# A fused decoder layer on one core: attention probabilities turned by VectorE and DMAs, an earlier last gate, smaller recurrence tiles, and side work that may lag further

## The chip, the cores and the metric

The kernel runs on one core of one Trainium2 chip. The metric is device time in microseconds (us) of one execution. The names of the engines are those of the profile: PE is TensorE (matmul; PEld its weight load), DVE is VectorE, ACT is ScalarE, POOL is GpSimd, SP is SyncE, whose queue here only issues DMAs.

## The reference

One layer of a decoder over 256 positions and 2048 channels, in float32. One wide product of the normalised input gives everything that three branches and the gates need. Cut to its core:

```python
hn = rms_norm(h, ln_gain[l])
z = split_columns(hn @ w_in[l] + b_in[l])
y_a = rglru_branch(z['lru_x'], ...) * silu(z['lru_gate'])          # linear recurrence
y_b = nsa_branch(q_b, k_c, v_c, k_s, v_s, k_w, v_w, g_b) * silu(z['nsa_gate'])   # sparse attention, 8 heads
y_c = fox_branch(q, k, v, log_f) * silu(z['fox_gate'])             # attention with forget bias, 8 heads
mg = sigmoid(z['merge']).reshape(b, s, 3, D_MODEL)
merged = (mg[:, :, 0] * (y_a @ w_branch[l, 0])
          + mg[:, :, 1] * (y_b @ w_branch[l, 1])
          + mg[:, :, 2] * (y_c @ w_branch[l, 2]))
h = h + merged @ w_out[l]
e = rms_norm(p[l] @ w_ple[l], ple_gain[l])
h = h + sigmoid(h @ w_ple_gate[l]) * e
```

In the two attention branches softmax probabilities of a block of 128 queries are multiplied with the values. For the sparse branch there are a window part and a selected part (each 128 or 256 keys wide, for the first and the second block of queries) and a small compressed part.

## The kernel before, in words

**Products.** Every float32 operand is held as two parts, a high part (names ending in h: `wh`, `k_yh`, `k_hnh`) and a low part (`wl`, `k_yl`, `k_hnl`), and a product is three matmuls: high by high, high-of-weight by low, low by high. The weights are read once as a stream of some 390 "halves" of at most 128 x 1024 numbers. SP loads a half into `raw` (5 buffers); ACT copies it into `wh`, DVE subtracts to get `wl` (4 buffers of each, three halves ahead of use, in `cut`); PE then does 12 matmuls of 128x512 on it (`by_rows`), into one of two pairs of PSUM banks (`main`). This stream is PE's main work, and `plan()` (lines 88 to 150) writes its order out: the recurrence's inputs and gate, the sparse attention's inputs with its gate, then 12 merge chunks `c`, each with its gate product (`merge`) and its branch product (`proj`), four chunks per branch, then the output product and the last gate. The forgetting attention's inputs come before the merge chunk 4. Each `proj` half names which quarter of the split branch output `ysplit0` to `ysplit2` it needs.

**Side work.** Everything else is written as Python generators that are woven into that stream (`Side`): `lru_task` (4 of them, the recurrence), `nsa_task` (8, sparse attention, two heads and one block of 128 queries each), `fox_task` (8, one head each), `turn_chunk` (a gate or the recurrence input turned to channels on partitions), `y_split` (a branch output times its gate, split into `k_yh` and `k_yl` in four pieces). At each half and in the middle of it, `tick` lets tasks emit their next instructions, first the urgent ones and then the others, as long as a planner's estimate says that DVE and ACT lag behind PE by no more than `LIMITS`, 3.0 us for urgent tasks and 2.0 for the others. When a half needs something that isn't emitted yet (`need`), tasks are run regardless. `room` and `give` count tiles of three pools (`k4`: 4 KB per partition, 5 tiles; `k2`: 11 tiles; `k1`: 8 tiles), `settle` lets PE go on until other engines should be done, `landed` waits 7 us of planned time for a DMA. All of this is decided when the program is built; on the chip each engine runs its own list in order. All instructions are recorded by one helper and so bear line 206 in the profile; the tiles tell them apart.

**Turning.** There are two ways to transpose. On PE, a 128x128 block is multiplied with the identity into a PSUM bank (`bank<-cst,...` in the profile). Or `cross`: DVE turns all 32x32 blocks of a tile in one instruction into `zt`, and four DMAs on SP's queue move the blocks in runs of 128 bytes to where they belong. In `before`, `cross` serves the gates, the recurrence input, the keys, the queries and the merged sum; the probabilities are turned on PE. `cells` and `celled` are views of a tile in the order in which `cross` needs it.

**The start.** `row_scales` sums the squares of the input over the partitions with small matmuls on a tile of ones, and raises the result to the power of minus a half on POOL; the first chunks wait for the outcome, `rsr`.

Of the kernel before, what the change touches and what calls it, by code (L numbers as in the profile page):

```python
# [76 lines left out]
def plan():  # L77
# [50 lines left out]
    for c in range(12):  # L128
        b, j = divmod(c, 4)
        if c == 4:  # L130
            for i, r in enumerate(rows(5, N_SIDE)):
                if i == 0:
                    r[0]["starts"] = ("ysplit1",)
                out += r
        for i, q in enumerate(rows(N_SIDE + c, N_SIDE + c + 1)):
            if j == 0 and b != 1:
                q[0]["starts"] = (f"ysplit{b}",)
            out += q
        out += item("proj", c, 8, 512, ("w_branch", b, [(512 * j, 512)]),
                    needs=lambda k, b=b: (f"ysplit{b}{k // 2}",))  # L140
# [183 lines left out]
def block_kernel(ctx: ExitStack, tc: tile.TileContext, io):  # L324
# [54 lines left out]
    def split(hi, lo, src, scale=None):  # L379
        splits((hi, lo, src, scale))  # L380
# [102 lines left out]


    A.activation(sml([P, 8], name="tbl"), half_n, AF.Copy)
    def issue_x(h, k=0, n=2):

        if "pair" in h:
            i = h["pair"]
            if i + k == 0:  # L490
                Q.dma_start(x0, io["x0"])
            else:
                Q.dma_start(x_pair(i)[:, k:k + n, :], io["xT"][:, 2 * i + k:2 * i + k + n])
# [62 lines left out]
    def row_scales(acc):  # L556

        yield from side.settle()
        b, = yield from side.take()
        for t in range(NT):  # L560
            for i in range(2):
                T.matmul(banks[b][:, 2 * t:2 * t + 2], acc[:, i, t * P:(t + 1) * P], ones[:, :2],
                         start=i == 0, stop=i == 1)
        yield True
        r = sml([P, 4], name="rsc")
        rsqrt(r, banks[b][:, :4], D)
        side.back(b)
        yield from side.powers()
        V.tensor_copy(rsr, r.rearrange("p (t i) -> p t i", i=2)[:, :, 0])

# [85 lines left out]

    def cross(dst, src):


        zt = mid([P, 4, 8, 32], name="zt")  # L660
        if type(src) is list:
# [13 lines left out]
    def turn_chunk(read, out, into, dst, k0, name):  # L675
# [37 lines left out]
    def lru_task(i):  # L713
        yield from side.wait("vec", f"lru_x{i // 2}")
        yield from side.room(k2=4, k4=2)
        u = st["u"]
# [26 lines left out]
        for c in range(2):  # L743
            for s in range(2):
# [3 lines left out]
                T.matmul(g, wdl[:, c, s, :], ucs[c][:, s, :], start=False, stop=True)  # L748
        side.give(k4=2)
        yield True  # L750
# [131 lines left out]
    def nsa_task(g, pr, t):  # L882
# [10 lines left out]
        G.memset(pc3, 0.0)  # L893
        p = mid([P, 2, 2, n * P], name="prob")

        def soft(a, sc):

            for i, (o, x, msk) in enumerate(zip((pc[:, a, :], p[:, a, 0, :], p[:, a, 1, :]), sc,
                                                (cmask[:, t, :], mask[:, P * (2 - n):2 * P], mask[:, P:P + n * P]))):
# [36 lines left out]
        at = [banks[bs[0]][:, :256], banks[bs[0]][:, 256:]] if t == 0 else [banks[x] for x in bs]  # L936
# [58 lines left out]
    def fox_task(h):  # L995
        c = h // 4
        yield from side.wait(f"fq{c}", f"fk{c}", f"fv{c}", "forget", "vec")
        fq, fk, fv = st["fq"], st["fk"], st["fv"]
        yield from side.room(k1=5, k2=2)
        nck = one([P, S], name="nck")  # L1000
# [12 lines left out]
        side.give(k1=5)  # L1013
        p = two([P, 3 * P], name="fprob")
        m, s = sml([P, 2], name="fm"), sml([P, 2], name="fs")
        cols = (slice(0, P), slice(P, 3 * P))
        for t in range(NT):
            V.tensor_tensor_reduce(p[:, cols[t]], banks[b][:, cols[t]], bias[:, cols[t]], -1.0, FLOOR,
                                   OP.add, OP.min, m[:, t:t + 1])
            A.activation(p[:, cols[t]], p[:, cols[t]], AF.Exp, bias=m[:, t:t + 1], scale=-1.0, accum_out=s[:, t:t + 1])  # L1020
        side.back(b)
        side.give(k2=1)
        yield True
        yield from side.room(k1=2, k2=2)
        V.tensor_scalar(s, s, 1e-30, None, op0=OP.max)
        V.reciprocal(s, s)
        for t in range(NT):
            V.tensor_scalar(p[:, cols[t]], p[:, cols[t]], s[:, t:t + 1], None, op0=OP.mult)
        vh, vl = (one([P, S], R32, name="fx") for _ in range(2))
        split(vh, vl, fv[:, h].rearrange("p t d -> p (t d)"))  # L1030
        yield from side.settle()
        b, = yield from side.take()

        for i in range(3):
            T.transpose(banks[b][:, i * P:(i + 1) * P], p[:, i * P:(i + 1) * P], ident)
        yield True
        pth, ptl = two([P, 3 * P], R32, name="fpth"), two([P, 3 * P], R32, name="fptl")
        split(pth, ptl, banks[b][:, :3 * P])
        side.back(b)
        side.give(k2=1)  # L1040
# [214 lines left out]
    for i, h in enumerate(halves):  # L1255
# [11 lines left out]
        if "pair" in h:  # L1267
            squares(h["pair"], xacc)
            if h["pair"] == 7:
                side.urge("rs", row_scales(xacc))  # L1270
        if i == 5:
# [70 lines left out]
LAND = 7000.0  # L1342
LIMITS = 3000.0, 2000.0

# [76 lines left out]
```

## Time and profile before

| what | value |
|---|---|
| median of 3 runs | 1092.37 us (1091.62 to 1093.23) |
| profiled execution, its own time | 1091.14 us |
| its span | 1089.4 us |
| mean granted clock | 0.993 |
| DVE busy | 762.3 us (70%) |
| ACT busy | 612.3 us (56%) |
| DMA packets, of these under 512 B | 159368, 103097 |

A row of a group has the operation, out<-in and how often it occurs, then its busy time, the mean of one in ns, and the idle time before it with what ended that. A timeline row has start, duration, what, and in brackets the idle time before it with what ended it. A row of the table by stretches has, after the stretch, its length, then the busy time of PE, PEld, DVE, ACT and POOL with the number of instructions, then the granted clock, the DMA share and GB/s. Matmuls overlap, so the cost of one is the distance from its start to the next start, not its duration.

### The profile page before, as it was taken

To read this page: it belongs to the slowest core of one execution; us is meant where nothing else is said; L and a number is where in the kernel's file an instruction comes from. 1 tells how busy PE (TensorE), PEld (TensorE's weight loads), DVE (VectorE), ACT (ScalarE), POOL (GpSimd) and SP (SyncE) were. 2 spreads that over 40 slices of the span, in tenths; PEclk is the share of its full clock that TensorE was granted. 3 is DMA by queue.
4 is the path that set the end of the run, shared out by engine and by line. 5 is a ranking of instruction groups with operands and counts; after the bars stand their busy time and mean duration, and the time that the engine had idled before them with its cause. 6 is when DMAs were issued, how large, how long until landed. Compare 5 with 4: busy or idle time off the path is not lost.

```text
span 1089.4 us, 14109 instructions
## 1 busy us (share of the span) xinstructions
PE 1069.4 (98%) x5019; PEld 892.5 (82%) x5019; DVE 762.3 (70%) x1119; ACT 612.3 (56%) x912; POOL 52.1 (5%) x77
## 2 busy tenths in 40 slices
PE   9999999999979999999999999999989999999998
PEld 8788898878768888888888888888868888888886
DVE  7787788977676678677787855565665666676654
ACT  7569975587855556554555544455554544444442
POOL 0000001100000000011110000000000100000000
PEclk9999999999989999999999999999989999999999
DMA  9767868878746556459667566777747887888772
GB/s 338 227 212 242 252 201 267 268 225 230 209 128 188 168 165 175 145 158 274 201 205 224 188 193 185 231 222 213 211 136 246 248 257 210 238 239 253 270 230 78
DMA packets 159368, 232.82 MB, mean 214 GB/s; under 512 B 103097, under 2 KB 104257, under 8 KB 159297
## 3 DMA queue, kind: packets, MB, share of 16 engines
q1 hardware_dynamic: 154576, 216.16, 64.6%
q0 software_dynamic: 4720, 15.76, 5.1%
q8 instruction: 39, 0.64, 0.3%
q14 instruction: 33, 0.26, 0.1%
HBM read 215.62 MB, written 4.20 MB: 202 GB/s over the span
## 4 chain that ended last, share of the span: by engine, by line
PE 90%; ACT 2%; DVE 1%; issue 1%; DMA 0%; SPq 0%; ACTq 0%; DVEq 0%
PE main L206 84%; PE bank L206 5%; ACT wh L206 1%; DVE wl L206 0%; DMA raw<-in_w 0%; SPq L206 0%; ACT k_th L206 0%; ACT k_lru L206 0%; ACT L206 0%; DVE k_mg L206 0%; ACT k_gn L206 0%; DVE k_fin L206 0%; ACT k_yh L206 0%; DVE k_fq L206 0%; ACT k_gf L206 0%
## 5 line engine op out<-in xcount | busy, mean ns | idle before, releaser
L206 DVE TENSOR_TENSOR wl<-raw,wh 128x1024 fp32r<-128x1024 f32 (+2 forms) x388 | 462.3, 1201 | 273.7 <-ACT wh L206 272.2
L206 ACT ACTIVATE wh<-raw 128x1024 fp32r<-128x1024 f32 (+2 forms) x388 | 400.8, 1040 | 343.7 <-PE main L206 282.9
L206 PE MATMUL main<-wh,k_hnh 128*128 128x512 f32 (+2 forms) x1026 | 396.4, 387 | 0.9 <-ACT k_z L206 0.9
L206 PE MATMUL main<-wl,k_hnh 128*128 128x512 f32 (+2 forms) x1026 | 393.1, 384 | 0.5 <-DVE wl L206 0.4
L206 PE MATMUL main<-wh,k_hnl 128*128 128x512 f32 (+1 forms) x1024 | 392.5, 383 | 0.0
L206 PEld LDWEIGHTS main<-wh,k_hnh 128*128 128x128 f32 x1026 | 193.0, 188 | 37.5 <-ACT k_z L206 1.8
L206 PEld LDWEIGHTS main<-wh,k_hnl 128*128 128x128 f32 x1024 | 192.3, 188 | 38.0
L206 PEld LDWEIGHTS main<-wl,k_hnh 128*128 128x128 f32 x1026 | 193.1, 189 | 36.7 <-DVE wl L206 1.5
L206 PE MATMUL main<-wh,k_yh 128*128 128x512 f32 x192 | 77.0, 401 | 12.9 <-ACT k_yh L206 12.9
L206 PE MATMUL main<-wl,k_yh 128*128 128x512 f32 x192 | 76.3, 398 | 0.0
L206 PE MATMUL main<-wh,k_yl 128*128 128x512 f32 x192 | 76.2, 397 | 0.0
L206 PEld LDWEIGHTS main<-wh,k_yh 128*128 128x128 f32 x192 | 37.1, 193 | 21.1 <-ACT k_yh L206 13.7
L206 PE MATMUL main<-wh,k_mth 128*128 128x512 f32 x128 | 49.8, 389 | 0.0
L206 PE MATMUL main<-wl,k_mth 128*128 128x512 f32 x128 | 49.8, 389 | 0.0
L206 PE MATMUL main<-wh,k_mtl 128*128 128x512 f32 x128 | 49.8, 389 | 0.0
L206 PE MATMUL main<-wh,k_hth 128*128 128x512 f32 x128 | 49.8, 389 | 0.0
L206 PE MATMUL main<-wl,k_hth 128*128 128x512 f32 x128 | 49.8, 389 | 0.0
L206 PE MATMUL main<-wh,k_htl 128*128 128x512 f32 x128 | 49.8, 389 | 0.0
L206 PEld LDWEIGHTS main<-wh,k_yl 128*128 128x128 f32 x192 | 37.0, 192 | 8.3 <-DVE k_yl L206 0.4
L206 PEld LDWEIGHTS main<-wl,k_yh 128*128 128x128 f32 x192 | 37.1, 193 | 7.7
L206 ACT ACTIVATE k_mg<-k_mg 128x512 f32<-128x512 f32 x24 | 15.1, 632 | 25.3 <-DVE k_mg L206 25.1
L206 PEld LDWEIGHTS main<-wl,k_mth 128*128 128x128 f32 x128 | 24.0, 188 | 5.0
(249 smaller groups left out, 964.2 us busy)
## 6 DMA issues: line engine op xcount, KB each, us to landing
raw<-in_w SPq DMA_DIRECT2D x369, 512.0 KB, 4.4
bias<-in_b_in POOLq DMA_DIRECT2D x21, 256.0 KB, 4.1
raw<-in_w SPq DMA_DIRECT2D x8, 408.0 KB, 4.0
e_dram<-k_e POOLq DMA_DIRECT2D x4, 512.0 KB, 3.6
k_merged<-k_zt SPq DMA_DIRECT2D x16, 128.0 KB, 3.4
k_xc<-in_x POOLq DMA_DIRECT2D x4, 512.0 KB, 5.3
k_hx<-k_zt SPq DMA_DIRECT2D x16, 128.0 KB, 3.6
k_ec<-e_dram POOLq DMA_DIRECT2D x4, 512.0 KB, 7.6
```

Source lines behind the costliest of these rows:

```text
L206: r = call(out, *args, **kw)
```

## The change

1. **Probabilities by `cross`.** In `nsa_task` and `fox_task` the exponentials are written in cell order (`k_pz`, `k_fpz`), scaled there, and turned by `cross`, with the old probability tile as the blocks' buffer; the 72 transposes on PE go (4 tasks x 4, 4 x 8, and 8 x 3), and 16 DVE turns and 64 DMAs on SP's queue come. The high and low parts of the probabilities are then made from SBUF instead of PSUM, in one instruction where there were two. A sparse task takes two `k4` tiles at its start instead of one, a forgetting one three `k2` tiles instead of two.
2. **The last gate sooner.** `fox_gate`'s two chunks come behind merge chunk 6 instead of 7.
3. **Recurrence tiles.** The gate weights `wd` of a `lru_task` move from the `k4` pool to `k2`; the task waits for one `k4` tile instead of two.
4. **Limits.** 4.5 us for urgent tasks and 4.0 for the others.
5. **The start.** The first input `x0` is requested on ACT's queue instead of SP's. `squares` runs one half sooner. `row_scales` adds the two halves of the squares on DVE first and does two ones-matmuls instead of four (each float32 one is two PE instructions), and POOL writes `rsr` directly. `turn_chunk` emits its two copies without a break between.

```diff
-        if c == 7:
+        if c == 6:
             out += turned("fox_gate", needs=[f"fox{i}" for i in range(8)])
...
+    A.dma_start(x0, io["x0"])
+
...
     def row_scales(acc):
+        V.tensor_tensor(acc[:, 0, :], acc[:, 0, :], acc[:, 1, :], op=OP.add)
         yield from side.settle()
         b, = yield from side.take()
         for t in range(NT):
-            for i in range(2):
-                T.matmul(banks[b][:, 2 * t:2 * t + 2], acc[:, i, t * P:(t + 1) * P], ones[:, :2],
-                         start=i == 0, stop=i == 1)
-        yield True
-        r = sml([P, 4], name="rsc")
-        rsqrt(r, banks[b][:, :4], D)
+            T.matmul(banks[b][:, 2 * t:2 * t + 2], acc[:, 0, t * P:(t + 1) * P], ones[:, :2], start=True, stop=True)
+        yield True
+        rsqrt(rsr, banks[b][:, :4].rearrange("p (t i) -> p t i", i=2)[:, :, 0], D)
...
-        yield from side.room(k2=4, k4=2)
+        yield from side.room(k2=4, k4=1)
...
-        wd = mid([P, 2, 2, P], name="wd")
+        wd = two([P, 2, 2, P], name="wd")
...
-        yield from side.room(k1=3, k4=1)
+        yield from side.room(k1=3, k4=2)
...
-        p = mid([P, 2, 2, n * P], name="prob")
+
+        p, pz = mid([P, 4, 4 * n, 32], name="prob"), mid([P, 4, 4 * n, 32], name="pz")
...
-            for i, o in enumerate((pc[:, a, :], p[:, a, 0, :], p[:, a, 1, :])):
-                A.activation(o, o, AF.Exp, bias=m[:, a, i:i + 1], scale=-1.0, accum_out=s[:, a, i:i + 1])
+            for i, (o, x) in enumerate(((pc[:, a, :], pc[:, a, :]), (cell[:, a, 0], cells(ps[:, a, 0, :])),
+                                        (cell[:, a, 1], cells(ps[:, a, 1, :])))):
+                A.activation(o, x, AF.Exp, bias=m[:, a, i:i + 1], scale=-1.0, accum_out=s[:, a, i:i + 1])
...
-                V.tensor_scalar(p[:, a, w, :], p[:, a, w, :], s[:, a, 1 + w:2 + w], None, op0=OP.mult)
+                V.tensor_scalar(cell[:, a, w], cell[:, a, w], s[:, a, 1 + w:2 + w], None, op0=OP.mult)
+        pt = pz.rearrange("p b n j -> p (b n j)")
+        yield from cross(pt, pt, p)
+        side.give(k4=1)
         yield from side.room(k4=2)
-        yield from side.settle()
-        bs = yield from side.take(n)
...
-        for a in range(2):
-            for i in range(2 * n):
-                c = i % n * P
-                T.transpose(at[a][:, i * P:(i + 1) * P], p[:, a, i // n, c:c + P], ident)
-        yield True
...
-        splits(*((pth[:, :, a, :], ptl[:, :, a, :], at[a].rearrange("p (i q) -> p i q", q=P), None) for a in range(2)))
-        side.back(*bs)
+        split(*(x.rearrange("p i a q -> p (i a q)") for x in (pth, ptl)), pt)
...
-LIMITS = 3000.0, 2000.0
+LIMITS = 4500.0, 4000.0
```

`fox_task` changes in the same way as `nsa_task`.

How the order of instructions moves, at three places. First ACT before the first branch's product, in `before`; `k_mg` is the tanh of merge chunk 0, `k_th` and `k_gn` the sparse branch's gate, `k_yh` the pieces of the first branch:

```order
L206 ACTIVATE k_mg_2904<-k_mg_2904 128x512
L206 ACTIVATE k_mg_2905<-k_mg_2905 128x512
L206 ACTIVATE wh_2912<-raw_2819 128x1024
L206 ACTIVATE k_th_2916<-k_gn_2499,vec 128x256
L206 ACTIVATE k_gn_2499<-k_gn_2499,vec 128x256
L206 ACTIVATE k_th_2920<-k_gn_2499,vec 128x256
L206 ACTIVATE k_gn_2499<-k_gn_2499,vec 128x256
L206 ACTIVATE k_yh_2924<-k_yl_558 128x512
```

The first piece stands behind the tanh pair, a weight copy and four gate instructions. The same stretch of ACT in the changed kernel, from the third piece on:

```order
L206 ACTIVATE k_yh_2791<-k_yl_559 128x512
L206 ACTIVATE wh_2870<-raw_2802 128x1024
L206 ACTIVATE k_th_2886<-k_gn_2542,vec 128x256
L206 ACTIVATE k_gn_2542<-k_gn_2542,vec 128x256
L206 ACTIVATE k_th_2890<-k_gn_2542,vec 128x256
L206 ACTIVATE k_gn_2542<-k_gn_2542,vec 128x256
L206 ACTIVATE wh_2896<-raw_2829 128x1024
L206 ACTIVATE wh_2914<-raw_2847 128x1024
```

Three pieces now stand ahead of the gate and of the tanh pair (which follows, after four more gate instructions); the fourth comes two weight copies behind that pair. Second, ACT before the third branch's product in `before`, where `k_mg` is the tanh of merge chunk 8:

```order
L206 ACTIVATE k_yh_2924<-k_fq_4375 128x512
L206 ACTIVATE wh_7012<-raw_6937 128x1024
L206 ACTIVATE k_mg_7028<-k_mg_7028 128x512
L206 ACTIVATE k_mg_7029<-k_mg_7029 128x512
L206 ACTIVATE wh_7036<-raw_6963 128x1024
L206 ACTIVATE wh_7054<-raw_6989 128x1024
L206 ACTIVATE k_yh_2924<-k_fq_4375 128x512 x3
```

One piece comes ahead of the tanh pair and three behind it. In the changed kernel:

```order
L206 ACTIVATE k_yh_2791<-k_fq_4333 128x512 x2
L206 ACTIVATE wh_6928<-raw_6858 128x1024
L206 ACTIVATE k_yh_2791<-k_fq_4333 128x512
L206 ACTIVATE wh_6951<-raw_6884 128x1024
L206 ACTIVATE k_yh_2791<-k_fq_4333 128x512
L206 ACTIVATE wh_6972<-raw_6902 128x1024
L206 ACTIVATE wh_6990<-raw_6926 128x1024
L206 ACTIVATE wh_7008<-raw_6949 128x1024
L206 ACTIVATE wh_7026<-raw_6970 128x1024
L206 ACTIVATE k_mg_7042<-k_mg_7042 128x512
```

All four pieces stand ahead of the tanh pair, with four weight copies between. Third, SP's queue early in the sparse attention of the changed kernel, where `before` has weight loads alone:

```order
L206 DMA raw_3087<-in_w 128x1024
L206 DMA k_pz_2643<-k_prob_2642 128x4x32 x4
L206 DMA raw_3127<-in_w 128x1024
L206 DMA raw_3145<-in_w 128x1024
L206 DMA raw_3163<-in_w 128x1024
L206 DMA k_pz_2656<-k_prob_2655 128x8x32 x4
L206 DMA raw_3189<-in_w 128x1024
```

The four DMAs of a cross stand between weight loads, three loads apart here.

More of the change, by code (lines that the diff above doesn't have):

```diff
@@ L489, in issue_x @@
             i = h["pair"]
-            if i + k == 0:
-                Q.dma_start(x0, io["x0"])
-            else:
+            if i + k:
                 Q.dma_start(x_pair(i)[:, k:k + n, :], io["xT"][:, 2 * i + k:2 * i + k + n])
@@ L560, in row_scales @@
         for t in range(NT):
-            for i in range(2):
-                T.matmul(banks[b][:, 2 * t:2 * t + 2], acc[:, i, t * P:(t + 1) * P], ones[:, :2],
-                         start=i == 0, stop=i == 1)
+            T.matmul(banks[b][:, 2 * t:2 * t + 2], acc[:, 0, t * P:(t + 1) * P], ones[:, :2], start=True, stop=True)
         yield True
-        r = sml([P, 4], name="rsc")
-        rsqrt(r, banks[b][:, :4], D)
+        rsqrt(rsr, banks[b][:, :4].rearrange("p (t i) -> p t i", i=2)[:, :, 0], D)
         side.back(b)
         yield from side.powers()
-        V.tensor_copy(rsr, r.rearrange("p (t i) -> p t i", i=2)[:, :, 0])
     hn = [(big([P, 8, S], R32, name="hnh"), big([P, 8, S], R32, name="hnl")) for _ in range(2)]
@@ L655, in celled, with cross @@
         return [z[:, :, :, t, :] for t in range(NT)]
-    def cross(dst, src):
-        zt = mid([P, 4, 8, 32], name="zt")
+    def cross(dst, src, zt=None):
+        if zt is None:
+            zt = mid([P, 4, 8, 32], name="zt")
         if type(src) is list:
@@ L748, in lru_task @@
                 T.matmul(g, wdl[:, c, s, :], ucs[c][:, s, :], start=False, stop=True)
-        side.give(k4=2)
+        side.give(k4=1)
         yield True
@@ L893, in nsa_task @@
         G.memset(pc3, 0.0)
-        p = mid([P, 2, 2, n * P], name="prob")
+        p, pz = mid([P, 4, 4 * n, 32], name="prob"), mid([P, 4, 4 * n, 32], name="pz")
+        ps = p.rearrange("p b n j -> p (b n j)").rearrange("p (a w k) -> p a w k", a=2, w=2)
+        cell = pz.rearrange("p b (w k a) j -> p a w b k j", w=2, a=2)
         def soft(a, sc):
-            for i, (o, x, msk) in enumerate(zip((pc[:, a, :], p[:, a, 0, :], p[:, a, 1, :]), sc,
+            for i, (o, x, msk) in enumerate(zip((pc[:, a, :], ps[:, a, 0, :], ps[:, a, 1, :]), sc,
                                                 (cmask[:, t, :], mask[:, P * (2 - n):2 * P], mask[:, P:P + n * P]))):
                 V.tensor_tensor_reduce(o, x, msk, -1.0, FLOOR, OP.add, OP.min, m[:, a, i:i + 1])
-            for i, o in enumerate((pc[:, a, :], p[:, a, 0, :], p[:, a, 1, :])):
-                A.activation(o, o, AF.Exp, bias=m[:, a, i:i + 1], scale=-1.0, accum_out=s[:, a, i:i + 1])
+            for i, (o, x) in enumerate(((pc[:, a, :], pc[:, a, :]), (cell[:, a, 0], cells(ps[:, a, 0, :])),
+                                        (cell[:, a, 1], cells(ps[:, a, 1, :])))):
+                A.activation(o, x, AF.Exp, bias=m[:, a, i:i + 1], scale=-1.0, accum_out=s[:, a, i:i + 1])
         if t == 0:
@@ L931, in nsa_task @@
             for w in range(2):
-                V.tensor_scalar(p[:, a, w, :], p[:, a, w, :], s[:, a, 1 + w:2 + w], None, op0=OP.mult)
+                V.tensor_scalar(cell[:, a, w], cell[:, a, w], s[:, a, 1 + w:2 + w], None, op0=OP.mult)
+        pt = pz.rearrange("p b n j -> p (b n j)")
+        yield from cross(pt, pt, p)
+        side.give(k4=1)
         yield from side.room(k4=2)
-        yield from side.settle()
-        bs = yield from side.take(n)
-        at = [banks[bs[0]][:, :256], banks[bs[0]][:, 256:]] if t == 0 else [banks[x] for x in bs]
-        for a in range(2):
-            for i in range(2 * n):
-                c = i % n * P
-                T.transpose(at[a][:, i * P:(i + 1) * P], p[:, a, i // n, c:c + P], ident)
-        yield True
         pth, ptl = mid([P, 2 * n, 2, P], R32, name="pth"), mid([P, 2 * n, 2, P], R32, name="ptl")
-        splits(*((pth[:, :, a, :], ptl[:, :, a, :], at[a].rearrange("p (i q) -> p i q", q=P), None) for a in range(2)))
-        side.back(*bs)
+        split(*(x.rearrange("p i a q -> p (i a q)") for x in (pth, ptl)), pt)
         side.give(k4=1)
@@ L998, in fox_task @@
         fq, fk, fv = st["fq"], st["fk"], st["fv"]
-        yield from side.room(k1=5, k2=2)
+        yield from side.room(k1=5, k2=3)
         nck = one([P, S], name="nck")
@@ L1013, in fox_task @@
         side.give(k1=5)
-        p = two([P, 3 * P], name="fprob")
+        p, pz = two([P, 4, 3, 32], name="fprob"), two([P, 4, 3, 32], name="fpz")
+        pt = pz.rearrange("p b n j -> p (b n j)")
         m, s = sml([P, 2], name="fm"), sml([P, 2], name="fs")
         cols = (slice(0, P), slice(P, 3 * P))
+        cell = (pz[:, :, :1], pz[:, :, 1:])
         for t in range(NT):
-            V.tensor_tensor_reduce(p[:, cols[t]], banks[b][:, cols[t]], bias[:, cols[t]], -1.0, FLOOR,
-                                   OP.add, OP.min, m[:, t:t + 1])
-            A.activation(p[:, cols[t]], p[:, cols[t]], AF.Exp, bias=m[:, t:t + 1], scale=-1.0, accum_out=s[:, t:t + 1])
+            x = p.rearrange("p b n j -> p (b n j)")[:, cols[t]]
+            V.tensor_tensor_reduce(x, banks[b][:, cols[t]], bias[:, cols[t]], -1.0, FLOOR, OP.add, OP.min, m[:, t:t + 1])
+            A.activation(cell[t], cells(x), AF.Exp, bias=m[:, t:t + 1], scale=-1.0, accum_out=s[:, t:t + 1])
         side.back(b)
@@ L1023, in fox_task @@
         yield True
-        yield from side.room(k1=2, k2=2)
         V.tensor_scalar(s, s, 1e-30, None, op0=OP.max)
@@ L1027, in fox_task @@
         for t in range(NT):
-            V.tensor_scalar(p[:, cols[t]], p[:, cols[t]], s[:, t:t + 1], None, op0=OP.mult)
+            V.tensor_scalar(cell[t], cell[t], s[:, t:t + 1], None, op0=OP.mult)
+        yield from cross(pt, pt, p)
+        side.give(k2=1)
+        yield from side.room(k1=2, k2=2)
         vh, vl = (one([P, S], R32, name="fx") for _ in range(2))
         split(vh, vl, fv[:, h].rearrange("p t d -> p (t d)"))
[L1031 to L1036, printed above, removed]
         pth, ptl = two([P, 3 * P], R32, name="fpth"), two([P, 3 * P], R32, name="fptl")
-        split(pth, ptl, banks[b][:, :3 * P])
-        side.back(b)
+        split(pth, ptl, pt)
         side.give(k2=1)
@@ L1266, in block_kernel @@
             ready += 1
[L1267 to L1270, printed above, removed]
+        for g in halves[:1] * (i == 0) + halves[i + 1:i + 2]:
+            if "pair" in g:
+                squares(g["pair"], xacc)
+                if g["pair"] == 7:
+                    side.urge("rs", row_scales(xacc))
         if i == 5:
```

## Prediction

> **What bounds the kernel now.** I read the page first, then the table of waits, then PE's timeline at the two longest waits, then a table by stretches of time.
>
> From the page: busy time by engine, the granted clock in 40 slices, and the shares of the chain that ended last.
>
> ```profile
> PE 1069.4 (98%) x5019; PEld 892.5 (82%) x5019; DVE 762.3 (70%) x1119; ACT 612.3 (56%) x912; POOL 52.1 (5%) x77
> PEclk9999999999989999999999999999989999999999
> PE 90%; ACT 2%; DVE 1%; issue 1%; DMA 0%; SPq 0%; ACTq 0%; DVEq 0%
> ```
>
> TensorE is the bound: 98% busy and 90% of the chain. So only two things change the time: work that leaves TensorE, and time in which TensorE waits or runs at a lower clock. VectorE has 30% of the span free, ScalarE 44%. The waits name the largest one, and PE's timeline shows its two occurrences (start, duration, what; the bracket is the idle time before).
>
> ```profile
> PE main L206 <- ACT k_yh L206: 12.9, 2, 8.4
> ...
> 297.40 0.39 PE L206 MATMUL main<-wl,k_hnh 128*128 128x512 f32 x1
> 297.63 0.39 PE L206 MATMUL main<-wh,k_hnl 128*128 128x512 f32 x1
> 306.38 0.80 PE L206 MATMUL main<-wh,k_yh 128*128 128x512 f32 x1 [8.36 <-ACT k_yh L206]
> ...
> 309.92 0.39 PE L206 MATMUL main<-wh,k_yl 128*128 128x512 f32 x1
> ```
> ```profile
> 791.15 0.39 PE L206 MATMUL main<-wh,k_yl 128*128 128x512 f32 x1
> 796.08 0.80 PE L206 MATMUL main<-wh,k_yh 128*128 128x512 f32 x1 [4.54 <-ACT k_yh L206]
> ...
> 801.36 0.41 PE L206 MATMUL main<-wh,k_yh 128*128 128x512 f32 x1
> ```
>
> A 128x512 matmul normally starts 0.23 us after the one before it (297.40 to 297.63). At the first wait the step is 8.75 us, 8.52 too much. The next eight steps, to 309.92, take 3.54 us where eight normal ones take 1.84: 1.70 too much, because the clock is still low. At the second wait the step is 4.93 us, 4.70 too much, and the twelve steps to 801.36 take 5.28 where 2.76 is normal: 2.52 too much. Together 8.52 + 1.70 + 4.70 + 2.52 = **17.4 us**. The table by stretches has the clock (column before the DMA share):
>
> ```profile
> 302.20:309.00 6.80, 2.62 (x6) 2.10 (x7) 4.79 (x13) 4.80 (x14) 0.26 (x1) 0.56 0.45 149
> 793.80:800.60 6.80, 4.52 (x11) 3.52 (x12) 4.71 (x7) 1.89 (x3) 0.00 (x0) 0.56 0.51 154
> ```
>
> Both stretches have 0.56, where the page has 0.9 or more nearly everywhere.
>
> **The two stalls.** What TensorE waits for there are the split halves of a branch output, made on VectorE and ScalarE behind other work:
>
> ```profile
> 305.69 0.63 ACT L206 ACTIVATE k_yh<-k_yl 128x512 fp32r<-128x512 f32 x1 [1.09 <-DVE k_yl L206]
> ...
> 795.39 0.63 ACT L206 ACTIVATE k_yh<-k_fq 128x512 fp32r<-128x512 f32 x1 [2.08 <-DVE k_fq L206]
> ...
> L206 ACT ACTIVATE wh<-raw 128x1024 fp32r<-128x1024 f32 (+2 forms) x388 | 400.8, 1040 | 343.7 <-PE main L206 282.9
> ```
>
> In the new order three of the first branch's four pieces stand ahead of the merge chunk's tanh and the fourth only two weight copies and the tanh pair behind; all four of the third branch stand ahead of that tanh. The cause of the first is that the last recurrence task and the gate get their tiles sooner (wd in the smaller pool), of the second that fox_gate comes one merge chunk sooner. What is late next is the first branch's fourth piece. TensorE wants it after three halves of the projection, 3 x 12 x 0.23 = 8.3 us after the start; ScalarE's work from the tanh pair on is two copies of 1.04 us and three instructions of the piece's width, 0.63 each: 4.0 us, so it is there unless VectorE is over 4 us late. I take all **-17.4**. If one stall stays, 7.2 to 10.2 comes back (a rival below).
>
> **Transposes off TensorE.** 48 transposes of the sparse-attention probabilities and 24 of the forgetting attention's leave it. From PE's timeline, one run of each size with what follows:
>
> ```profile
> 327.94 0.60 PE L206 MATMUL bank<-cst,k_prob 128*128 128x128 f32 x4
> 328.29 0.48 PE L206 MATMUL main<-wh,k_hnh 128*128 128x512 f32 x1
> 328.60 0.40 PE L206 MATMUL main<-wl,k_hnh 128*128 128x512 f32 x1
> ...
> 456.56 1.04 PE L206 MATMUL bank<-cst,k_prob 128*128 128x128 f32 x8
> 457.36 0.36 PE L206 MATMUL bank<-k_pth,k_vv 128*128 128x256 f32 x1
> ...
> 533.61 0.49 PE L206 MATMUL bank<-cst,k_fprob 128*128 128x128 f32 x3
> 533.86 0.48 PE L206 MATMUL main<-wh,k_hnh 128*128 128x512 f32 x1
> ```
> ```profile
> L206 PE MATMUL bank<-cst,k_prob 128*128 128x128 f32 x48 | 6.5, 272 | 0.0
> ...
> L206 PE MATMUL bank<-cst,k_fprob 128*128 128x128 f32 x24 | 3.9, 272 | 0.0
> ```
>
> Four take 0.35 us to the next start and lengthen that step from 0.23 to 0.31: 0.43. Eight take 0.80. Three take 0.25 and, with the same 0.08 behind them, 0.33. With four tasks of four, four of eight and eight of three: 1.7 + 3.2 + 2.6 = **-7.5**. (The busy sum, 10.4, counts overlaps twice.)
>
> What replaces them is 16 turns on VectorE and 64 DMAs on SyncE's queue, four per turn, as the weight loads are.
>
> ```profile
> L206 DVE STREAM_TRANSPOSE k_zt<-k_merged 128x1024 f32<-128x1024 f32 x4 | 5.0, 1245 | 0.1
> L206 DVE TENSOR_TENSOR k_htl<-k_hx,k_hth 128x512 fp32r<-128x512 f32 x8 | 5.1, 683 | 0.0
> L206 DVE TENSOR_TENSOR k_qn<-k_z,sp_nss 128x512 f32<-128x512 f32 x4 | 4.1, 1072 | 0.0
> ...
> 290.00:460.00 170.00, 161.64 (x800) 135.74 (x799) 120.09 (x280) 96.72 (x205) 3.98 (x11) 0.98 0.54 163
> ```
>
> By width, 1.245 us for 1024 columns, the turns cost 4 x 1.25 + 4 x 0.62 + 8 x 0.47 = 11.2 us of VectorE. The exponentials and scalings on cell order have no row; the nearest pair above is 0.683 contiguous against 1.072 with permuted operands, so between nothing and 1.6 times. VectorE is idle for 50 us and ScalarE for 73 in the 170 us of the sparse attention; that cover takes either end, and I cost it at nothing. Without the cover all 11.2 would come back. The wait for landing delays only the task itself.
>
> The queue is the doubtful part. SyncE issues in order, so weight loads stand behind a cross whose transpose isn't done:
>
> ```profile
> 545.86 5.58 SPq L206 DMA_DIRECT2D k_fq<-k_zt  x4
> ...
> ACT wh L206 <- DMA raw<-in_w: 16.7, 14, 4.1
> ...
> L206 PE MATMUL main<-wl,k_hnh 128*128 128x512 f32 (+2 forms) x1026 | 393.1, 384 | 0.5 <-DVE wl L206 0.4
> ```
>
> The four DMAs of one cross took 5.58 us to issue, and the weight loads next on the queue that much longer; ScalarE has waited up to 4.1 us for a raw weight; yet TensorE lost 0.4 us in all to late low halves. So lateness of 4.1 us is covered today. The bounds are 0 and the slower rival's price; I take one uncovered hold, 5.58 - 4.1 = **+1.5**.
>
> **Side work may lag further.** The limits rise by 1.5 us for urgent tasks and 2.0 for the others. That is what makes the pieces earlier, and it is taken from the lead of the weight splits. In the dense early stretches that lead is already used up at three places, the first and the last of them here with the second:
>
> ```profile
> 161.26 0.39 PE L206 MATMUL main<-wl,k_hnh 128*128 128x272 f32 x1
> ...
> 185.37 0.50 PE L206 MATMUL main<-wl,k_hnh 128*128 128x512 f32 x1
> ...
> 226.97 0.50 PE L206 MATMUL main<-wl,k_hnh 128*128 128x512 f32 x1 [0.17 <-DVE wl L206]
> ...
> 100.00:200.00 100.00, 99.93 (x569) 87.58 (x568) 80.25 (x112) 77.14 (x112) 4.78 (x5) 1.00 0.80 246
> ```
>
> Each is a matmul that starts just as its low half arrives; the last sat idle 0.17 us for it. With 2.0 us more lag each stalls up to 2.0. Below, 0: TensorE's delay at one place is lead at the next, and the engines have 20% free to catch up. Above: three places in 66 us are one per 33 with both ends taken as one, so nine over the 300 us of dense stretches, 18 us. I take the three that the trace shows, at full price: **+6**.
>
> Does such a stall also halve the clock? Idle times of 4.54 and 8.36 do, 0.17 doesn't; 2.0 lies nearer the lower end, so I add nothing; else 1.7 to 2.5 more each, 5 to 8 for three. [...]
>
> **Small edits.** The row scales arrive sooner, with four ones-matmuls instead of eight, and the first input is requested from ScalarE's queue.
>
> ```profile
> 51.03 0.50 PE L206 MATMUL main<-wh,k_hnh 128*128 128x512 f32 x1 [0.49 <-ACT k_z L206]
> ...
> L206 PE MATMUL bank<-ones,k_xacc x8: 165/251/251, 44.0 to 44.7; 128*128 128x2 f32 x8
> ...
> 0.74 0.39 SPq L206 DMA_DIRECT2D x<-in_x  x1
> 1.19 0.89 SPq L206 DMA_DIRECT2D raw<-in_w  x2
> ```
>
> Eight starts in 0.7 us are 0.1 each: -0.4. The wait of 0.49 goes, **-0.5**; bounds 0 and twice that, for a like wait behind it. The first weights start 0.45 us sooner, but ScalarE's table load follows the issue (0.39): from -0.45 to +0.39, taken at -0.3.
>
> **The sum.** -17.4 - 7.5 - 0.4 - 0.5 - 0.3 = -26.1; +6 + 1.5 = +7.5; net -18.6. The profiled execution took 1091.14 us, so 1072.5; it lies 1.2 below the median of the runs, 1092.37, so I forecast **1074**. Differences below 0.2%, 2.2 us, can hardly be told from no change.
>
> **The rivals.**
> - *The lag costs nothing* (at most 3 us given back): 1092.37 - 26.1 = 1066.3, up to 1070. For it: VectorE and ScalarE recover within a few halves. Against: 226.97 shows no lead left. 0.20.
> - *The lag bites everywhere*: 18 instead of 6, 1086; 1079 to 1086. For it: 77 to 80% busy side engines. Against: the trace shows three places. 0.13.
> - *The stall isn't gone*: the change doesn't do what it says at one of the two places, because the pieces now stand ahead in the order but still wait for VectorE. Adds 7.2 to 10.2: 1081 to 1084. For it: the second stall's piece waited 2.08 for VectorE, not for ScalarE's queue. 0.12.
> - *The crosses starve the weights* (slower). All 16 hold SyncE's queue, each for up to the 4.1 us that ScalarE already waits, with the cover cut by the 2.0 of new lag: 4.1 - (4.1 - 2.0) = 2.0 each, 33 us, and nothing else goes wrong: 1092.37 - 26.1 + 33 = 1099. It decides from 26.1 / 16 = 1.6 us per cross. For it: the held queue at 545.86. Against: the crosses there today cost TensorE 0.4 at most in all, and a DMA share of 0.54 in the stage. 0.05. [...]
>
> **How the numbers follow.** My forecast, 4 to 12 us given back (1070 to 1079), has 0.47; 0.20 for the clean case, 0.13 and 0.12 for the next two, 0.05 slower, and 0.03 that several of them together end within 0.2%. Faster: 0.47 + 0.20 + 0.13 + 0.12 = 0.92. The range is 1065 to 1086: the clean case less the runs' spread at the bottom, the lag at its upper bound at the top; it leaves out 0.08 and the tails.
>
> **What would show it.** After: no wait of PE for k_yh over 1 us, no slice of the clock below 9; no k_prob transposes on PE; new waits of PE for wl or wh, 6 us in sum, between 100 and 290 us; ScalarE's wait for raw above 16.7. Wrong, if PE still waits for k_yh, or waits for wl by more than 12 us in all, or for wl behind late raw loads in the attention stages.

## The result, and the profile after

The changed kernel takes 1074.5 us (median of 4 runs, 1073.41 to 1075.94), the kernel before 1092.36 (1091.62 to 1093.23): a ratio of 0.9837, 95% interval 0.982 to 0.9854. The profiled execution took 1075.37 us with a span of 1073.6; against the profiled execution of before that is 15.8 us less, by the medians 17.9.

From the page of the changed kernel, busy time by engine and the granted clock; then all that PE waited for:

```profile
PE 1061.1 (99%) x4943; PEld 884.0 (82%) x4943; DVE 770.2 (72%) x1127; ACT 619.1 (58%) x905; POOL 51.9 (5%) x77
PEclk9999999999999999999999999999999999999999
```
```profile
PE main L206 <- DVE wl L206: 3.7, 6, 0.8
PE main L206 <- ACT wh L206: 2.1, 3, 0.7
PE bank L206 <- PEq L1408: 0.8, 1, 0.8
PE main L206 <- DVE kk L206: 0.2, 1, 0.2
```

The wait for `k_yh`, 12.9 us before, is gone altogether. In its place stand nine short waits for the high and low parts of weights. One of them, 0.57 us, lies ahead of the first product; the others lie almost all before 200 us, as the table by stretches shows (after the stretch and its length: busy PE, PEld, DVE, ACT, POOL; clock, DMA share, GB/s):

```profile
100.00:200.00 100.00, 94.97 (x526) 81.27 (x525) 76.96 (x114) 77.42 (x119) 4.35 (x6) 0.98 0.75 230
290.00:460.00 170.00, 170.00 (x816) 142.71 (x815) 131.14 (x277) 104.21 (x195) 3.71 (x10) 1.00 0.68 198
530.00:640.00 110.00, 110.00 (x512) 91.93 (x512) 83.21 (x136) 59.23 (x91) 9.37 (x13) 1.00 0.76 221
```

In the two attention stages, where the new turns are, PE is now busy all the time. The turns are not the reason: the 8.36 us that the stretch from 290 us lacked before (161.64 of 170) are the first stall, which ended at 306.38 us. From 100 to 200 us it is the other way round: 99.93 busy before, 94.97 now. The three largest places there, from PE's timeline:

```profile
122.09 0.39 PE L206 MATMUL main<-wh,k_hnl 128*128 128x512 f32 x1
123.22 0.50 PE L206 MATMUL main<-wh,k_hnh 128*128 128x512 f32 x1 [0.74 <-ACT wh L206]
124.48 0.50 PE L206 MATMUL main<-wl,k_hnh 128*128 128x512 f32 x1 [0.76 <-DVE wl L206]
...
166.51 0.39 PE L206 MATMUL main<-wl,k_hnh 128*128 128x272 f32 x1 [0.83 <-DVE wl L206]
...
188.02 0.39 PE L206 MATMUL main<-wh,k_hnl 128*128 128x512 f32 x1
189.15 0.51 PE L206 MATMUL main<-wh,k_hnh 128*128 128x512 f32 x1 [0.75 <-ACT wh L206]
190.41 0.50 PE L206 MATMUL main<-wl,k_hnh 128*128 128x512 f32 x1 [0.76 <-DVE wl L206]
...
194.39 0.39 PE L206 MATMUL main<-wh,k_hnl 128*128 128x512 f32 x1
```

Each pair takes 2.39 us for two steps that normally take 0.46: 1.9 us. After the second pair the ten steps to 194.39 take 3.98 us where 2.30 is normal, 1.7 more, because the clock is low:

```profile
190.40:194.40 4.00, 3.99 (x11) 3.13 (x12) 4.00 (x7) 3.14 (x5) 0.54 (x1) 0.57 0.95 377
```

The two places have different causes. ScalarE's timeline at each, and SyncE's queue before the second (this view begins behind the first two of the cross's four issues; all four took 6.52 us):

```profile
116.94 1.28 ACT L206 ACT_TABLE_LOAD   x1
118.24 3.85 ACT L206 ACTIVATE k_lru<-bank,vec 64x256 f32<-64x256 f32 x8
122.11 3.91 ACT L206 ACTIVATE wh<-raw 128x1024 fp32r<-128x1024 f32 x4
```
```profile
188.04 1.06 ACT L206 ACTIVATE wh<-raw 128x1024 fp32r<-128x1024 f32 x1 [4.26 <-DMA raw<-in_w]
```
```profile
178.78 4.36 SPq L206 DMA_DIRECT2D k_zn<-k_zt  x2
183.23 7.49 SPq L206 DMA_DIRECT2D raw<-in_w  x6
```

At 117 to 122 us the recurrence's sigmoids and a table load, 5.1 us, stand ahead of the weight copies: side work that lags. At 188 us ScalarE has nothing to do; the raw weight is late, and ahead of it on SyncE's queue stood the cross of the sparse attention's keys, which is no part of the change. The kernel before issues that cross too, for 5.12 us from 172.67 us, and PE doesn't wait behind it. So the held queue makes a wait only together with the lead that the change has used up.

The new work itself, by groups; the same exponential in the profile of before; and the start of the changed kernel (ScalarE's first work, PE's first product):

```profile
L206 DVE STREAM_TRANSPOSE k_prob<-k_pz 128x1024 f32<-128x1024 f32 x4 | 5.0, 1246 | 0.1
...
L206 DVE STREAM_TRANSPOSE k_fprob<-k_fpz 128x384 f32<-128x384 f32 x8 | 4.6, 579 | 0.3
...
L206 ACT ACTIVATE k_pz<-k_prob,sp_m 128x256 f32<-128x256 f32 x16 | 11.9, 744 | 0.0
```
```profile
L206 ACT ACTIVATE k_prob<-k_prob,sp_m 128x256 f32<-128x256 f32 x16 | 8.0, 502 | 0.0
```
```profile
3.81 0.51 ACT L206 ACTIVATE k_hnh<-x 128x256 fp32r<-128x256 f32 x1 [1.14 <-DMA x<-in_x]
...
4.68 1.22 PE L206 MATMUL main<-wh,k_hnh 128*128 128x256 f32 x4 [0.57 <-ACT wh L206]
```

An exponential of 256 columns in cell order takes 744 ns instead of 502. PE's first product starts at 4.68 us; in the profile of before it started at 3.96.

### The profile page after: what moved, and what is told of

It is laid out like the page before. It is cut to its first block, busy times and chain, and to the rows that moved or that the text cites. A ratio compares the mean times of both kernels' runs of the same rounds, so it can differ in the third digit from the quotient of the medians.

```text
span 1073.6 us, 14079 instructions
## 1 busy us (share of the span) xinstructions
PE 1061.1 (99%) x4943; PEld 884.0 (82%) x4943; DVE 770.2 (72%) x1127; ACT 619.1 (58%) x905; POOL 51.9 (5%) x77
## 4 chain that ended last, share of the span: by engine, by line
PE 88%; ACT 4%; DVE 4%; issue 2%; DMA 1%; SPq 1%; ACTq 0%; DVEq 0%
PE main L206 84%; PE bank L206 4%; ACT wh L206 2%; DVE wl L206 2%; DMA raw<-in_w 1%; SPq L206 1%; ACT k_lru L206 1%; ACT L206 0%; ACT k_gl L206 0%; ACT k_th L206 0%; DVE k_uc L206 0%; DVE k_yl L206 0%; DVE k_qn L206 0%; DVE k_z L206 0%; DVE k_fq L206 0%
## 5 line engine op out<-in xcount | busy, mean ns | idle before, releaser
L206 PEld LDWEIGHTS main<-wh,k_mth 128*128 128x128 f32 x128 | 24.0, 188 | 5.0
```

The lines of the kernel that those rows point to most:

```text
L206: r = call(out, *args, **kw)
```

## The experiments

All times are medians; the ratios are to the kernel before, run on the same chip with each group. "Before" is 1091.9 to 1092.5 in all four groups. The changed kernel was not run again beside them, so a difference from its 1074.5 us is one between groups. A short stretch of low clock, which in the changed kernel followed one of two like pairs of waits and not the other (last section), is worth 1.7 us; differences of less than 2 us between two medians therefore say little by themselves, and the traces have to decide. Where "PE's starts" are named, the start of the same product of the weight stream is compared in two traces.

| run | us | ratio, 95% interval |
|---|---|---|
| gate_only | 1085.86 | 0.9943, 0.9928 to 0.9958 |
| limits_only | 1097.75 | 1.0051, 1.0034 to 1.0067 |
| tiles_limits | 1092.35 | 1.0001, 0.9992 to 1.001 |
| pe_turns | 1081.82 | 0.99, 0.9882 to 0.9918 |
| gate_back | 1080.77 | 0.9896, 0.9883 to 0.991 |
| low_limits | 1088.11 | 0.9972, 0.9959 to 0.9984 |
| low_then_high | 1082.35 | 0.9911, 0.9894 to 0.9927 |
| staged_limits | 1068.48 | 0.9782, 0.9769 to 0.9796 |
| old_scales | 1073.76 | 0.983, 0.9815 to 0.9845 |
| x0_on_sp | 1072.95 | 0.9831, 0.9818 to 0.9845 |
| keys_other_queue | 1071.38 | 0.981, 0.9795 to 0.9824 |
| staged_other_queue | 1067.76 | 0.9775, 0.9759 to 0.9792 |

### What made the two long stalls go

**gate_only**, the kernel before with one edit:

```diff
-        if c == 7:
+        if c == 6:
```

> The kernel before with fox_gate's chunks behind merge chunk 6, nothing else of the change. Theory (the gate's place makes the second stall): the wait of PE for k_yh near 791 us goes with its low clock, 7.2 us, so 1085; the first, near 298 us, stays. Rival (the raised limits made it go): both stalls stay, 1092.

6.1 us faster. PE's wait for `k_yh` is left at one place, the first:

```profile
PE main L206 <- ACT k_yh L206: 8.4, 1, 8.4
```

**gate_back** takes that one edit out of the changed kernel.

> The changed kernel with fox_gate's chunks behind merge chunk 7 again. Theory (the gate's place makes the second stall, whatever the limits): a wait for k_yh of 4 to 4.5 us near 780 us, with or without the low clock, 1079 to 1082. Rival (with the raised limits it would have gone anyway): 1074.5.

1080.77, 6.3 us slower, and the wait is back:

```profile
789.32 0.79 PE L206 MATMUL main<-wh,k_yh 128*128 128x512 f32 x1 [4.35 <-ACT k_yh L206]
```

The gate's place makes the second stall, with the old limits and with the new. By PE's starts the second place alone is worth 7.3 us in gate_only: ahead of it this run is 2.0 us behind the kernel before, behind it 5.2 us in front.

**limits_only**, the kernel before with

```diff
-LIMITS = 3000.0, 2000.0
+LIMITS = 4500.0, 4000.0
```

> The kernel before with the limits 4.5 and 4.0 us, nothing else of the change. Theory of the prediction (the first stall goes by the smaller recurrence tile, the second by the gate's place; the limits only bring lag): both stalls stay and the short waits for wl and wh of the changed kernel, 9.2 us with their low clock, come on top, about 1101. Rival (the limits alone let the pieces of both branches be ready): both stalls go, 1092.4 - 17.4 + 9.2 = 1084.

Slower than before by 0.5%. What PE waits for:

```profile
PE main L206 <- DVE wl L206: 8.6, 8, 3.2
PE main L206 <- ACT wh L206: 4.0, 4, 1.7
PE main L206 <- ACT k_yh L206: 3.8, 1, 3.8
```

Neither theory had this. The wait for `k_yh` at the first place is gone, but at the same place PE now waits 5 us for the weights' parts, the longest waits of the first two rows. ScalarE and VectorE there:

```profile
306.84 3.88 ACT L206 ACTIVATE wh<-raw 128x1024 fp32r<-128x1024 f32 x4
```
```profile
310.35 3.49 DVE L206 TENSOR_TENSOR wl<-raw,wh 128x1024 fp32r<-128x1024 f32 x3
```

From 296.3 to 306.84 us ScalarE copies no weight. The pieces stand there, but also reads of the gate and a softmax of the sparse attention; VectorE turns the gate and scales probabilities before its three splits. So the pieces come early enough, and they and other side work push the weights back. At the second place 3.8 us stay.

**tiles_limits**, the same with the smaller recurrence tile:

```diff
-        yield from side.room(k2=4, k4=2)
+        yield from side.room(k2=4, k4=1)
...
-        wd = mid([P, 2, 2, P], name="wd")
+        wd = two([P, 2, 2, P], name="wd")
...
-        side.give(k4=2)
+        side.give(k4=1)
...
-LIMITS = 3000.0, 2000.0
+LIMITS = 4500.0, 4000.0
```

> The kernel before with wd in the pool k2 and the limits 4.5 and 4.0 us; gate, crosses and start as before. Theory (limits and the smaller tile together make the first branch's pieces early): no wait over 1 us near 298 to 310 us, the second stall stays at 4 to 7 us, the short waits are as in the changed kernel: 1092 - 10.2 + 9 - 2 = 1089. Rival (the tile does nothing): as with the limits alone, 1098, with 5.7 us of waits for wh and wl near 306 us.

1092.35, 5.4 us faster than the limits alone, and no wait is left near 300 us; the second stall stays at 3.8 us, as expected. So with the raised limits it takes the smaller tile as well, or the weights are late in place of the pieces. That the tile doesn't do it with low limits is seen in low_limits, below; the tile with the old limits, 3.0 and 2.0, was not tried. The run is 3 us slower than I expected: it has more short waits for parts of weights than the changed kernel (7.9 us of idle time against 5.8), the longest, 1.60 us at 83.56 us, at a place where the changed kernel has none. From here to the run pe_turns, which is this with the gate moved (about 6.2) and the edits of the start and of turn_chunk, another 4.3 us go; they belong to those last edits together. Only two of them were undone singly (below); turn_chunk's removed break, which decides when the gates' chunks free their banks, was not tried alone.

### The turns

**pe_turns**: nsa_task and fox_task of before in the changed kernel.

```diff
-        yield from cross(pt, pt, p)
...
+                T.transpose(at[a][:, i * P:(i + 1) * P], p[:, a, i // n, c:c + P], ident)
...
+            T.transpose(banks[b][:, i * P:(i + 1) * P], p[:, i * P:(i + 1) * P], ident)
```

> The changed kernel with nsa_task and fox_task as before: 72 transposes on PE again, no crosses for probabilities. Theory: 7.5 us of PE time come back, 1082. Rival (the crosses cost in held weight loads about what they save): no difference, 1074.5. Rival (the short waits before 200 us come from the crosses): these waits vanish and it is below 1074.

7.3 us slower than the changed kernel by the medians (one of the four runs took only 1078.08 us), where 7.5 was expected. PE's starts give 8.1 over the two attention stages: pe_turns is 1.2 us in front at 309 us and 6.9 us behind at 735. The short waits stay much as they were:

```profile
PE main L206 <- DVE wl L206: 3.7, 6, 0.8
PE main L206 <- ACT wh L206: 2.2, 3, 1.1
```

So no cost of the crosses shows on PE, and they aren't the cause of the short waits. ScalarE does wait longer for raw weights with them, 25.6 us in all against 19.6, but that stays covered. Crosses of the probabilities in the kernel before, without the rest, were not tried.

### What makes the short waits

**low_limits**, the changed kernel with

```diff
-LIMITS = 4500.0, 4000.0
+LIMITS = 2500.0, 2000.0
```

> The changed kernel with limits 2.5 and 2.0 us. Theory (the short waits between 120 and 195 us and at 487 us are paid for the raised limits): these 9.2 us vanish, but the first branch's pieces come late again, 10.2 us near 298, so 1075.5, and the wait for k_yh is back in the trace. Rival (the short waits come from the tiles or the crosses): they stay and the stall comes on top, 1085.

1088.11, 13.6 us slower than the changed kernel. The wait for `k_yh` is back, as expected (9.0 us in all), but the short waits haven't vanished: one of them has become long. PE and VectorE there:

```profile
200.87 0.50 PE L206 MATMUL main<-wl,k_hnh 128*128 128x512 f32 x1 [4.69 <-DVE wl L206]
```
```profile
194.52 1.52 DVE L206 SCALAR_TENSOR_TENSOR k_uc<-k_u,vec,k_uc 128x255 f32<-128x255 f32 x3
195.96 0.88 DVE L206 SCALAR_TENSOR_TENSOR kk<-k_zn,vec,kk 128x256 fp32r<-128x256 f32 x2
...
199.60 3.49 DVE L206 TENSOR_TENSOR wl<-raw,wh 128x1024 fp32r<-128x1024 f32 x3
```

My theory fell for this run: lower limits do not remove the short waits. A block of recurrence and key work stands on VectorE ahead of three weight splits. In the code, `need` forces tasks in that a half waits for (here, as I read it, the reads of the `kk` and `vs` chunks), and a forced `tick` lets every task emit a step, whatever the lag. That this forcing makes the block is argued from the code and not shown; the next two runs show that it comes with early limits of 2.5 and 2.0 us and not with 3.5 and 2.5.

**low_then_high**, the low limits up to half 88 only (LIMITS being the changed kernel's), with x0 on SP's queue:

```diff
+        side.at = i
...
-                if self.clock.behind() > LIMITS[group is self.active] and not hurry:
+                if self.clock.behind() > self.limits()[group is self.active] and not hurry:
...
+    def limits(self):
+        return LIMITS if any(a <= self.at < b for a, b in LAG) else TIGHT
...
+TIGHT = (2500.0, 2000.0)
+LAG = ((88, 1000),)
```

> Limits 2.5 and 2.0 us up to half 88 of the weight stream, 4.5 and 4.0 from there; otherwise the changed kernel with x0 on SP's queue. Theory (limits that are too low early leave tasks that are then forced in where they are needed, and the forced block makes the wait of 4.7 us near 196 us): that wait stays, so that the waits for wl and wh before 235 us are 6 to 8 us, not fewer than with 3.5 and 2.5; the first branch's pieces come in time or nearly (under 2 us), about 1074. Rival (lower limits give shorter waits; what cost time with the low limits was the first branch's stall alone): waits under 3 us before 235 us, 1067.

1082.35. The wait of 4.7 us at that place stays, 6.0 us for low parts in all; and the first branch's pieces are late by 5.2 us, more than expected:

```profile
PE main L206 <- DVE wl L206: 6.0, 4, 4.7
PE main L206 <- ACT k_yh L206: 5.4, 2, 5.2
```

So low limits early cost both there and later: what is put off up to half 88 isn't made good by higher limits after it.

**staged_limits**: the same with other numbers.

```diff
-LAG = ((88, 1000),)
-TIGHT = (2500.0, 2000.0)
+LAG = ((76, 1000),)
+TIGHT = (3500.0, 2500.0)
```

> The changed kernel with limits 3.5 and 2.5 us up to half 76 of the weight stream (about 195 us) and 4.5 and 4.0 from there, and x0 back on SP's queue. Theory (the raised limits, where they act early, make the short waits; they are needed only from the last recurrence tasks on): most of the 8 us of waits for wl and wh before 195 us go, no wait for k_yh comes back, 1067. Rival (the waits come from the rest of the new order and from late raw loads): 5 us or more of them stay, 1073.

1068.48: 4.5 us faster than the same kernel with the high limits throughout (x0_on_sp, below), which has 3.8 and 3.6 us in the two rows.

```profile
PE main L206 <- DVE wl L206: 2.2, 4, 0.8
PE main L206 <- ACT wh L206: 1.4, 2, 1.1
PE bank L206 <- DVE wl L206: 0.9, 1, 0.9
```

The waits shrink from 7.4 us to 4.5; between 10 and 195 us, where the early limits act, from 5.1 to 1.6. No wait for `k_yh` returns. So much of the early lag isn't needed for the pieces. The pair at 188 us is among the waits that go: the cross of the keys is issued at 165.31 us here and at 175.16 in x0_on_sp. The next run takes that pair away in another manner.

**keys_other_queue**: the changed kernel with x0 on SP's queue, and norm_rows' crosses issued by POOL.

```diff
-            Q.dma_start(to[:, :, a, :], zt[32 * a:32 * a + 32].rearrange("p b n j -> p (b n) j"))
+            (queue or Q).dma_start(to[:, :, a, :], zt[32 * a:32 * a + 32].rearrange("p b n j -> p (b n) j"))
...
-        yield from cross(dst, dst)
+        yield from cross(dst, dst, queue=G)
```

> The changed kernel with x0 on SP's queue and the crosses of the normalised queries and keys (28 DMAs, k_zn, k_qn, k_fq, k_fk) issued from POOL's queue instead of SP's. Theory (the cross of the keys, whose four issues took 7.2 us near 175 us in the run with x0 on SP's queue, holds the weight loads behind it, and so makes ACT's wait for raw and PE's waits of 2.4 us near 188 us): these waits of PE go, 1070.5 against 1073 with x0 on SP's queue alone. Rival (the loads are late because the DMA engines are full there, share 1.01 at 186 to 190 us): the waits stay, 1073.

1071.38 (1071.28 to 1072.6), 1.6 us less than 1072.95 (1072.67 to 1076.4) without the edit; 2.4 was expected. The intervals of the ratios just overlap, so the time alone doesn't settle it; the place does. SyncE's queue without and with the edit, then PE at the place in question:

```profile
175.16 7.17 SPq L206 DMA_DIRECT2D k_zn<-k_zt  x4
182.43 7.42 SPq L206 DMA_DIRECT2D raw<-in_w  x6
```
```profile
188.29 0.49 PE L206 MATMUL main<-wh,k_hnh 128*128 128x512 f32 x1 [1.22 <-ACT wh L206]
189.55 0.50 PE L206 MATMUL main<-wl,k_hnh 128*128 128x512 f32 x1 [0.77 <-DVE wl L206]
```
```profile
170.93 19.94 SPq L206 DMA_DIRECT2D raw<-in_w  x11
...
187.04 0.39 PE L206 MATMUL main<-wh,k_hnh 128*128 128x512 f32 x1
187.26 0.39 PE L206 MATMUL main<-wl,k_hnh 128*128 128x512 f32 x1
```

The loads run on, and the same two products, now at 187.04 and 187.26 us, start without a wait; a wait of 0.21 us is new one half of weights earlier. By PE's starts the place gives 2.5 us, about as expected, of which 0.8 is lost again later. So the held queue was the cause of this pair. The rival, full DMA engines, falls: they are as full here from 178 to 182 us (share 1.02), and PE is busy there all the time.

**staged_other_queue**: both edits together.

> The kernel with staged limits and the same crosses on POOL's queue. Theory (held weight loads make what is left of the waits between 177 and 182 us, 2.3 us): 1066 against 1068.5. Rival (those waits are the side work's lag): 1068.5, or more if POOL's queue is slower for the tasks.

1067.76, the fastest of all. Its ratio, 0.9775 (0.9759 to 0.9792), can't be told from that of staged_limits. The two waits between 177 and 182 us (0.93 and 0.66) are gone, and one of 0.88 stands 10 us later, so neither theory is settled by this run.

### The start

**x0_on_sp** undoes the edit of the first request.

> The changed kernel with x0 requested on SP's queue again, ahead of the first weights. Theory (x0 lands 0.9 us later when its request doesn't stand ahead of the weights; the start of the changed kernel is 1.8 us behind in the profile): 1.0 to 1.8 us faster, 1073. Rival (the start differs by chance from execution to execution): no difference, 1074.5.

1072.95 against 1074.5; the intervals of the two ratios (0.9818 to 0.9845, 0.982 to 0.9854) overlap, so this is not shown in the time. In its trace PE is 1.0 us in front of the changed kernel at 10 us. It ends 2.4 us in front, but most of the rest comes at 189 us, where the changed kernel's trace happens to have the low clock and this one doesn't. All that can be said is that the edit of the first request brought no gain.

**old_scales**: row_scales and the place of squares as before.

> The changed kernel with row_scales and the place of squares as before. Theory: the two waits of PE for k_z near 50 us come back, 0.65 + 0.59 over the normal step, and 0.4 us of ones-matmuls: 1.6 us, 1076. Rival (the wait is hidden or moves to another place): no difference, 1074.5.

1073.76: no slower. One of the two waits of 0.5 us for `k_z` is back, the other isn't, and PE's starts show a loss of 1.3 us at the scales (0.7 us in front of the changed kernel at 41 us, 0.6 behind at 55). By 188 us it is made good, mostly because the changed kernel's wait at 155 us is missing, and the later pair at 189 us is shorter:

```profile
PE main L206 <- ACT k_z L206: 0.5, 1, 0.5
...
189.07 0.50 PE L206 MATMUL main<-wl,k_hnh 128*128 128x512 f32 x1 [0.45 <-DVE wl L206]
```
```profile
176.57 5.13 SPq L206 DMA_DIRECT2D k_zn<-k_zt  x4
```

PE comes to that place at the same time as in the changed kernel (188.01 and 188.02 us for the product ahead of it). But the cross of the keys was issued in 5.13 us instead of 6.52, ScalarE's copy of the late weight starts at 186.69 us instead of 188.04, and PE waits 0.45 us instead of 1.51, without the low clock behind it. A microsecond gained in one place can be lost in a wait for a load further on that the same edit moves; why the cross is shorter here was not looked for in a run of its own.

## Why the prediction was right

**The two stalls, -17.4: right.** No `k_yh` wait is left. The causes were the two that it named, with one addition: for the first stall the tile and raised limits are needed together (limits_only and low_limits against tiles_limits), so the limits aren't merely its price. In medians the gate's place was worth 6.1 and 6.3 us, at the place itself 7.3, where the profile gave 7.2.

**The turns, -7.5: right.** 7.3 measured by the medians, 8.1 by PE's starts. The cover on VectorE and ScalarE held: the turns took 12.5 us of VectorE where 11.2 was worked out, and the widest exponentials 1.5 times as long (744 against 502), inside the bound of 1.6.

**The crosses' hold, +1.5, and the rival that they starve the weights:** nothing that shows, for the new crosses (pe_turns). The mechanism exists, but it acts where an old cross meets a stage with no lead: at 188 us, 1.9 us and 1.7 of low clock. In that rival, sixteen holds of 2.0 us are 32 us and not 33; nothing hangs on it.

**The lag, +6: the stretch right, the places and the size not.** The waits lie before 290 us, as it said, but for one at 488. Of the three products that it named, only the first (161.26 us in the kernel before) waits now, at 166.51 us; the other two don't, and the pairs at 122 and 188 us were not among them. The one at 188 needs the held queue too. The nine waits have 5.8 us of idle time; what the eight behind the start cost is more, as each step is longer than its idle time: 1.9 at 122 us, 1.9 at 188, and with the rest some 7.7. With the 1.7 us of low clock it is 9.4. That term, "I add nothing" for the clock, failed: two waits of 0.75 us close together brought the low clock once.

**The start, -0.3: not borne out.** In the profiled execution PE's first product is 0.7 us later, because x0 landed later. That comes with the queue: in the five traces with the request on ScalarE's queue the first split of x0 starts at 3.7 to 3.9 us, in the nine others at 2.9 to 3.4. What it does to the whole time is not shown, as x0_on_sp is not shown to be faster. The rest of the 1.8 us is the low clock of the start: by the clock records full clock begins at 6.1 us in the trace of before and at 10.0 in that of after, and over all traces anywhere from 3.7 to 10.4. **The scales, -0.9:** the two waits are gone in the profile, and PE's starts show their worth at the place, but old_scales shows no gain in the time.

**The signs.** No slice of the clock is below 9, no `k_prob` transposes are left on PE, ScalarE's wait for raw weights rose from 16.7 to 25.6 us, and no wait for a late raw load stands in the attention stages. The new waits between 100 and 290 us have 4.6 us of idle time, where 6 was named.

**The sum.** With these sizes -17.4 - 7.3 - 1.6 (scales in the profile, 0.65 + 0.59 and the ones-matmuls) + 9.4 + 1.8 (the start with its low clock, which PE's steps show up to 10 us) = -15.1, where the two profiled executions differ by 15.8. PE's starts give the same stretches without any adding of waits (side work that has moved shifts them by up to a microsecond in between): +1.8 by 10 us, -2.0 over the scales, +10.5 from 55 to 200 us, -11.1 over the first stall, -8.2 over the attention stages, -7.3 at the second stall, -16.2 in all.

The predicted sum was -18.6, and the profiled executions differ by 2.8 us less: the lag and the start came out 3.4 and 2.1 us worse, the crosses' hold and the scales 1.5 and 0.7 better. That the forecast of 1074 lies only 0.5 us from the median is in part luck: the errors cancel in part, and the profiled execution, with its low clock at 190 us, was one of the two slower of the four.

## What to carry to other kernels

Price a stall with the slow steps after it (1.70 and 2.52 us at the two of the kernel before), and look for the one thing that the waiting piece stands behind: here two small edits, the gate's place and a tile's pool (with the raised limits), were worth 6 and 5 us. How far side work may lag is best set stage by stage; of the three early settings tried here, the middle one was the fastest. Too high, a limit eats the lead of the main stream where that is short; too low, work is put off and comes in a lump where it is due. And whatever shares a queue with the loads of the main stream needs lead there: in x0_on_sp the loads stood behind the 7.17 us of the keys' cross, and PE's waits of 1.22 and 0.77 us behind it went when the cross was issued by POOL.

## What the runs showed of the hardware that was not expected

The low clock came without one long wait. After 189.15 and 190.41 us, two waits of 0.75 and 0.76 us with a single matmul between, the mean clock of the next 4 us was 0.57; after the like pair of 0.74 and 0.76 us at 123.22 and 124.48 us it was 1.00 from 125 to 128 us. The prediction added nothing for the clock at waits of 2.0 us, as nearer to 0.17 us, which brought no drop, than to 4.54 and 8.36, which did; here no single wait was above 0.76 us, so that reading does not hold in this trace. The other traces bear on whether the size of the waits decides. All fourteen traces together have, behind the start, fourteen such pairs of 1.3 to 2.3 us of idle time. Of the nine up to 1.7 us two were followed by a drop, of the five longer ones four. So in these traces a longer pair brought the drop more often, but not surely. In pe_turns a pair of 1.08 and 0.76 us ended at 123.82 us; in x0_on_sp the longer one of 1.22 and 0.77 us, shown above, ended at 189.55. Right behind each the clock was 0.57 and 1.00:

```profile
124.50:128.50 4.00, 4.00 (x12) 3.14 (x11) 3.34 (x5) 3.92 (x6) 0.00 (x0) 0.57 0.83 257
```
```profile
189.50:193.50 4.00, 3.95 (x17) 3.30 (x18) 4.00 (x7) 4.00 (x6) 0.54 (x1) 1.00 1.04 380
```

In the clock records the two drops inside the run of the kernel before last 6.83 us each (303.03 to 309.86 us and 794.55 to 801.38), and the one of the changed kernel 3.41 us (190.93 to 194.34), each at a clock of 0.50. Why the pair at 189 us brought a drop and the like one at 123 us did not is not shown.
